# Ordering the chunked scan of a hybrid RWKV-7/Conformer layer: from a fixed tick to a rough clock of the engines

## The chip, the core and the metric

The kernel runs on one core of one Trainium2 chip. The metric is the device time of one execution in microseconds (us). The core has a matrix engine (PE, with its weight loads shown apart as PEld), a vector engine (DVE), an activation engine (ACT), a general engine (POOL) and a queue that issues transfers (SP). Each engine works through its own instructions in order, and waits on semaphores for the others.

## What is computed

One layer over 256 context tokens and 2048 latent tokens of 1024 channels. Two branches read the same normalised input, and their outputs are gated, added and projected. Cut to what matters:

```python
p = h @ w_in                                   # 74 column tiles of 128
# branch a: two linear recurrences per head (forward and backward), 16 heads of 64
def step(s, inp):
    rt, wt, kt, vt, at, bt = inp
    sa = einsum('bhij,bhj->bhi', s, at)
    s_new = s * wt + sa[..., None] * bt + vt[..., None] * kt
    return s_new, einsum('bhij,bhj->bhi', s_new if inclusive else s, rt)
y_sum = y_forward + y_backward
y_a = (layernorm_per_head(y_sum) * lnx_w + lnx_b + bonus) * silu(g_a)
# branch b: depthwise convolution over 31 tokens
z = u * sigmoid(g); z = conv31(z) + conv_b
y_b = silu(layernorm(z)) * silu(g_b)
merged = sigmoid(m_a) * (y_a @ w_proj_a) + sigmoid(m_b) * (y_b @ w_proj_b)
x_new = x + gate * (merged @ w_out); return rmsnorm(x_new)
```

## The kernel before

The program has three parts. The first normalises the input, projects the columns that the recurrence needs, and writes its operands to DRAM; a part of the gate columns is projected there too. The third is the end of the merge and the output projection. The change is in the second part, the scan.

**The scan.** The recurrence is cut into chunks of 64 tokens. Heads go in 8 pairs, a pair has 36 chunks (the first 4 are context), forward and backward chunks go together (d = 0, 1): 288 chunks in all, in steps of 4. `chunk` (L885) is a chain of three links. PE multiplies the state `SV` with the chunk's operand into `px` (L890), and ACT copies it to `xs` (L892). PE multiplies `xs` with the inverted triangle `Tt` (L896), and ACT copies the result into `UV` (L898). PE forms the update `psy` (L912), and DVE adds it to the decayed state (L914), which the next chunk's `px` needs. The output `py` (L921, L922) is off the chain; every second chunk it is copied (ACT, L935) or added (DVE, L937) into `y`.

**What fills the waits.** `prep` prepares the next step's operands (transposes `pbk`, `pvt`, the score products `psc` and their masks). `readout` (L853), once for blocks 1, 2 and once for 0, 3 of a pair, normalises `y`, and loads `bo`, `vn`, `ga` on SP. `filler` gives one dense matmul of 512 columns at a time (`pg`, L359: the rest of the gate and convolution inputs), and its own rule gives convolution steps (L969 to L977, on DVE) at `NCV` = 2.2 for every 6 matmuls. When all of that is out, `conv_branch` takes over: norms, then the projection of branch b (`pp`, L1142), then, once the last pair's blocks 1 and 2 are read out, the first projection of branch a.

**What sets the order.** A counter. `chunk` and the main loop call `tick` nine times a chunk, at fixed places:

```python
want = min(cnt["n"] * NF // NEND, NF)
while cnt["done"] < want:
    next(fill, None)
    cnt["done"] += 1
for _ in range(CBN):
    if cbs:
        next(cbs[0], None)
```

so every place gets its even share of the 2600 filler steps until the tick that 82% of 288 x 8 gives, and after that up to 3 steps of `conv_branch` (`CBN`). Every third tick takes a piece of `prep`. `readout` is a plain function, written out whole behind its chunk. Behind the code a scheduler of the build moves instructions on each engine within a short distance, with the written order as its priority; the rows of the program's order below are what it made of each version.

## Time and profile before

| what | before |
|---|---|
| median of 3 runs (lowest to highest) | 4161.96 us (4157.28 to 4163.86) |
| the profiled execution: its own time, its span | 4172.02 us, 4170.3 us |
| PE busy, PEld busy | 3840.2 us (92%), 2300.7 us (55%) |
| DVE busy, ACT busy, POOL busy | 2950.2 us (71%), 2178.5 us (52%), 352.0 us (8%) |
| mean granted clock of PE | 0.960 of full |

The span runs from the first to the last instruction. Busy time is the time in which at least one instruction of an engine was under way. A matmul is shown from its start to its modelled end, and the next one starts long before that end.

### The profile page before, as it was taken

Reading aid. Unit: us, or ns where it says so; the run is one execution under the profiler, and the core shown is the slowest. Engines: PE = TensorE matmul, PEld = TensorE weight load, DVE = VectorE, ACT = ScalarE, POOL = GpSimd, SP = SyncE. Lnnn points to the kernel's source line nnn. Section 1 sums busy time; section 2 is a strip of 40 time slices with the busy share of each in tenths; the row PEclk is TensorE's granted clock in tenths of the full one; section 3 lists DMA queues with packets and bytes.
Section 4 is the critical chain, followed back from the end, with each engine's and each line's share of the span. In section 5 each row is a group of like instructions: output and inputs, shape, how many; then the busy total and the mean of one; then the engine's idle time right before and its main releaser. Section 6 shows DMA issues by size and latency. Waiting matters only on the chain. (4 is left out here: it accounts for less than half of the span.)

```text
span 4170.3 us, 78335 instructions
## 1 busy us (share of the span) xinstructions
PE 3840.2 (92%) x29008; PEld 2300.7 (55%) x29008; DVE 2950.2 (71%) x7226; ACT 2178.5 (52%) x4358; POOL 352.0 (8%) x874
## 2 busy tenths in 40 slices
PE   8999999998999997999999999999999898788999
PEld 3444444444444443776666667666666566675444
DVE  5577787788788686877887998895466773234644
ACT  5666665666666553445454454545555553335522
POOL 0000000000000000211111111111111000010000
PEclk9999999999999998999999999999999899699999
DMA  5343443444444343444334343446455554343522
GB/s 203 124 174 138 162 152 137 146 142 168 142 150 167 121 142 106 88 92 112 82 95 109 91 119 73 109 113 156 109 124 166 146 148 118 69 91 107 199 101 76
DMA packets 586117, 528.69 MB, mean 127 GB/s; under 512 B 375044, under 2 KB 439940, under 8 KB 585224
## 3 DMA queue, kind: packets, MB, share of 16 engines
q1 hardware_dynamic: 585736, 523.68, 43.5%
q8 instruction: 231, 3.78, 0.4%
q14 instruction: 150, 1.23, 0.1%
HBM read 298.01 MB, written 196.35 MB: 119 GB/s over the span
## 5 line engine op out<-in xcount | busy, mean ns | idle before, releaser
L359 PE MATMUL pg<-hH,whi 128*128 128x512 f16 x1536 | 592.9, 386 | 11.0 <-ACT whi L199 7.1
L359 PE MATMUL pg<-hH,wlo 128*128 128x512 f16 x1536 | 591.5, 385 | 1.4 <-DVE wlo L200 1.4
L359 PE MATMUL pg<-hL,whi 128*128 128x512 f16 x1536 | 592.1, 386 | 0.0
L914 DVE SCALAR_TENSOR_TENSOR SV<-psy,PL,pre 64x64 f32<-64x64 f32 x1120 | 316.4, 283 | 232.0 <-PE psy L912 211.2
L359 PEld LDWEIGHTS <-whi 128*128 128x128 f16 x3072 | 300.5, 100 | 267.7 <-issue 45.2
L904 POOL TENSOR_SCALAR pre<-SV,PL 128x128 f32<-128x128 f32 x560 | 285.3, 509 | 1863.9 <-DVE SV L914 1771.7
L892 ACT ACTIVATE xs<-px 128x256 f32<-128x256 f32 x288 | 110.1, 382 | 439.2 <-PE px L890 437.6
L977 DVE SCALAR_TENSOR_TENSOR acc<-z,cw,acc 128x512 f32<-128x512 f32 x464 | 331.2, 754 | 2.7
L208 PE MATMUL pg<-hH,whi 128*128 128x512 f16 x832 | 318.5, 384 | 4.2 <-ACT hH L278 4.1
L209 PE MATMUL pg<-hL,whi 128*128 128x512 f16 x832 | 318.8, 383 | 0.0
L210 PE MATMUL pg<-hH,wlo 128*128 128x512 f16 x832 | 318.5, 383 | 0.0
L842 PE MATMUL psc<-arz,bk 64*128 64x128 f32 (+1 forms) x2304 | 278.7, 297 | 12.5 <-ACT UV L836 8.5
L842 PEld LDWEIGHTS psc<-arz,bk 64*128 64x128 f32 x2304 | 228.9, 196 | 85.3 <-issue 47.7
L890 PE MATMUL px<-SV,arz 128*128 128x128 f32 x1152 | 230.0, 305 | 34.0 <-DVE SV L914 29.1
L845 DVE TENSOR_TENSOR arz<-psc,msk 64x256 f32<-64x256 f32 x288 | 120.7, 419 | 168.5 <-PE psc L842 164.5
L896 PE MATMUL px<-xs,Tt 128*128 128x128 f32 x1152 | 198.1, 295 | 40.7 <-ACT xs L892 40.1
L898 ACT ACTIVATE UV<-px 64x128 f32<-64x128 f32 x576 | 154.9, 269 | 150.8 <-PE px L896 147.1
L359 PEld LDWEIGHTS <-wlo 128*128 128x128 f16 x1536 | 153.0, 100 | 137.9 <-issue 23.6
L890 PEld LDWEIGHTS px<-SV,arz 128*128 128x128 f32 x1152 | 176.1, 199 | 93.1 <-DVE SV L914 31.0
L912 PE MATMUL psy<-UV,BK 128*128 128x128 f32 x1120 | 198.9, 301 | 28.8 <-ACT UV L898 28.6
L896 PEld LDWEIGHTS px<-xs,Tt 128*128 128x128 f32 x1152 | 166.3, 199 | 89.3 <-ACT xs L892 77.3
L921 PE MATMUL py<-arz,SV 128*128 128x128 f32 x1024 | 206.6, 285 | 4.4 <-ACT y L935 2.5
(374 smaller groups left out, 8151.4 us busy)
## 6 DMA issues: line engine op xcount, KB each, us to landing
wf<-in_w_in_dram SPq DMA_DIRECT2D x74, 512.0 KB, 3.8
arz<-arD SPq DMA_DIRECT2D x144, 256.0 KB, 4.8
bkD<-bk SPq DMA_DIRECT2D x64, 512.0 KB, 2.7
arD<-ar SPq DMA_DIRECT2D x64, 512.0 KB, 3.5
bk<-bkD SPq DMA_DIRECT2D x72, 256.0 KB, 3.8
bk<-bkD SPq DMA_DIRECT2D x144, 128.0 KB, 3.9
vvz<-vD SPq DMA_DIRECT2D x144, 128.0 KB, 2.8
lt<-loD SPq DMA_DIRECT2D x32, 512.0 KB, 4.8
```

The source lines that it names most:

```text
L208: PE.matmul(ps, whi[:, k, :], xhi(k), start=(k == 0), stop=False)
L209: PE.matmul(ps, whi[:, k, :], xlo(k), start=False, stop=False)
L210: PE.matmul(ps, wlo[:, k, :], xhi(k), start=False, stop=(k == NK - 1))
L359: PE.matmul(ps, wt[a][:, k, :], b[:, k, o:o + 512], start=(m == 0), stop=(m == 23))
L842: PE.matmul(ps[h][:, c, :ni, :], bk[hs, d, c, :], ar[hs, d, c, :ni, h, :], start=True, stop=True)
L890: PE.matmul(px[:, d, :], ar[:, d, c, 0].rearrange("p h l -> p (h l)"), SV[:, d, c, :], start=True, stop=True)
L896: PE.matmul(px[:, 2 + d, :], t[:, d, c, :], xs[:, d, :], start=True, stop=True)
L904: G.tensor_scalar(pr, SV[:, d, c, :], pl, 1.0, op0=ALU.mult, op1=ALU.mult)
L912: PE.matmul(psy, BK[:, d, c, :], UV[:, d, c, :], start=True, stop=True)
L914: V.scalar_tensor_tensor(Sn[hs, d, (c + 1) % 4, hs], psy[hs, hs], PL[hs, p, d, k + 1:k + 2], pre[d][hs, hs], op0=ALU.mult, op1=ALU.add)
L921: PE.matmul(o, SV[:, d, c, :], ar[:, d, c, 1].rearrange("p h l -> p (h l)"), start=True, stop=True)
L977: V.scalar_tensor_tensor(o, x[:, j:j + 512], cw[:, 2 * j + e:2 * j + e + 1], q if j == 0 else o, op0=ALU.mult, op1=ALU.add)
```

## The change

The code of every operation stays; where it is written changes.

- **A clock.** `Clocked` wraps PE, ACT and DVE while the program is written. It keeps a time in ns for each engine and a ready time for each tile, from a rule for each kind of instruction. It does not run on the chip.
- **Dense matmuls by need.** `tick` is gone. Behind each link `until(tile)` takes filler steps while PE's clock stands before the time at which the link's tile is ready, up to 30 (`MAXP`), and at most 24 steps ahead of the even share (`AHEAD`); behind each chunk the share is made up to 12 behind (`BEHIND`). The share now ends at 82% of the chunks: chunk 236, where it was tick 1889 of nine a chunk, chunk 210. `conv_branch` gives at least 16 steps a chunk (`MINCB`) and more where `until` asks.
- **y one chunk later.** `outputs` writes a chunk's `py` behind the next chunk's `px`.
- **Convolution behind state updates.** `conv_steps(lim)` writes convolution steps while DVE's clock is less than `lim` past PE's: 3200 behind the state update, 1200 and 500 in the other two links.
- **Readout and prep in pieces.** `readout` is a generator, one piece twice a chunk; `prep` yields after each copy of `SV` and `UV`.
- Smaller: `GF` 4 to 6 (which gate tiles come between the convolution's), weight tiles of the filler loaded further ahead, norm steps in `conv_branch` only while ACT's and DVE's clocks allow.

```diff
+            def call(*a, **kw):
+                aps = [q for q in list(a) + list(kw.values()) if is_ap(q)]
+                out, ins = (kw["out"], aps) if "out" in kw else (aps[0], aps[1:])
+                t = max([clk[self._n]] + [rdy.get(key(q), 0.0) + 35 for q in ins if wrt.get(key(q)) != self._n])
...
+                    d = (165 + 0.85 * n if ps else 90 + 1.06 * n) if self._n == "act" else 200 + 1.04 * n
+                    clk[self._n] = t + d - (90 if n > 64 else 0)
+                    rdy[key(out)] = t + d + 17
+                return fn(*a, **kw)
...
+    V, S, PE = Clocked(V, "dve"), Clocked(S, "act"), Clocked(PE, "pe")
...
     def chunk(p, k, e, t):
...
         S.activation(xs, px[:, 0:2, :], AF.Copy)
-        for _ in range(3):
-            tick()
+        scores_out()
+        if c == 0 and prv[0] is not None:
+            next(prv[0], None)
+        until(xs)
+        conv_steps(LIMA)
         for d in range(2):
             PE.matmul(px[:, 2 + d, :], t[:, d, c, :], xs[:, d, :], start=True, stop=True)
...
+        pieces(2 * c)
+        conv_steps(LIMB)
+        until(UV)
...
+        conv_steps(LIM)
+        pieces(2 * c + 1)
+        until(Sn)
...
+    def conv_steps(lim):
+        while convs and clk["dve"] < clk["pe"] + lim:
+            if next(convs[0], 1) == 1:
+                convs.pop(0)
+                cv["n"] += 1
...
-    def tick():
...
+    def pull():
+        if cbs:
+            cnt["cb"] += 1
+            return next(cbs[0], 1) is None
+        if cnt["done"] >= min(cnt["n"] * NF // NEND + AHEAD, NF):
+            return False
+        cnt["done"] += 1
+        next(fill, None)
+        return True
+
+    def until(t):
+        n = 0
+        while clk["pe"] < rdy.get(key(t), 0.0) + 35 and n < MAXP and pull():
+            n += 1
+
+    def pieces(gap):
+        if rd and next(rd[0], 1) == 1:
+            rd.pop(0)
+        want = max(0, gap - 1) * NPC // 6
+        while prv[0] is not None and cnt["pc"] < want:
+            cnt["pc"] += 1
+            next(prv[0], None)
```

Three places in the order of the program show what moves. In the changed version PE, ACT and DVE instructions of the scan all carry the line of the wrapper (L822).

The first is PE in chunk 124, in the middle of the scan; `pg` with its LDWEIGHTS is a dense filler matmul. Before, from the chunk's first link on:

```order
L890 MATMUL px<-SV_18651,arz_18649 128x128 x2
L359 LDWEIGHTS wlo
L359 MATMUL pg<-hH,wlo 128x512
L359 LDWEIGHTS whi
L359 MATMUL pg<-hH,whi 128x512
L359 LDWEIGHTS whi
L359 MATMUL pg<-hL,whi 128x512
L359 LDWEIGHTS wlo
L359 MATMUL pg<-hH,wlo 128x512
L896 MATMUL px<-xs,Tt_18647 128x128 x2
```

And in the changed version:

```order
L822 MATMUL px<-SV_18651,arz_18649 128x128 x2
L822 MATMUL py<-arz_18648,SV_18650 128x128
L822 MATMUL py<-sc,UV 128x128
L822 MATMUL py<-arz_18648,SV_18650 128x128
L822 MATMUL py<-sc,UV 128x128
L822 LDWEIGHTS whi
L822 MATMUL pg<-hL,whi 128x512
L822 MATMUL px<-xs,Tt_18647 128x128 x2
```

The four `py` of the chunk before now stand in the first link, which keeps one of its four dense matmuls; the third link, where `py` stood, has six where it had four.

The second is PE in chunk 268, late in the scan (the last pair), where `conv_branch` is what is left to fill with. Before, the whole chunk:

```order
L890 MATMUL px<-SV_18651,arz_18649 128x128 x2
L921 MATMUL py<-arz_18649,SV_18651 128x128
L896 MATMUL px<-xs,Tt_18647 128x128 x2
L912 MATMUL psy<-UV,BK 128x128 x2
L922 MATMUL py<-sc,UV 128x128
L921 MATMUL py<-arz_18649,SV_18651 128x128
L922 MATMUL py<-sc,UV 128x128
```

The changed version, the first rows of the same chunk (`pp` is the projection of branch b):

```order
L822 MATMUL px<-SV_18651,arz_18649 128x128 x2
L822 MATMUL py<-arz_18648,SV_18650 128x128
L822 MATMUL py<-sc,UV 128x128
L822 MATMUL py<-arz_18648,SV_18650 128x128
L822 MATMUL py<-sc,UV 128x128
L822 MATMUL px<-xs,Tt_18647 128x128 x2
L822 LDWEIGHTS wHb
L822 MATMUL pp<-xhi,wHb 128x512
L822 LDWEIGHTS wHb
L822 MATMUL pp<-xlo,wHb 128x512
L822 LDWEIGHTS wLb
L822 MATMUL pp<-xhi,wLb 128x512
```

A chunk that held no dense matmul now holds 12 of `pp`: 5 before `psy`, and 7 behind it in the link of the state update.

The third is ACT where the second pair's blocks 0 and 3 are read out (chunk 72); `sqy` is the readout's variance tile, and a table load goes before its logarithm and before its exponential. Before, up to the `xs` that the chain waits for:

```order
L858 ACTIVATE y<-pc 128x512
L866 ACT_TABLE_LOAD
L866 ACTIVATE sqy<-sqy 128x512
L860 ACTIVATE sqy<-y 128x512
L199 ACTIVATE whi<-wf,p2s 128x1024
L877 ACTIVATE y<-y,par 128x512
L863 ACT_TABLE_LOAD
L863 ACTIVATE sqy<-pv,eps 128x512
L829 ACTIVATE BK<-pbk 128x512
L866 ACT_TABLE_LOAD
L866 ACTIVATE sqy<-sqy 128x512
L892 ACTIVATE xs<-px 128x256
```

And in the changed version:

```order
L822 ACTIVATE xs<-px 128x256
L822 ACTIVATE UV<-px 64x2x64 x2
L822 ACT_TABLE_LOAD
L822 ACTIVATE sqy<-pv,eps 128x512
L822 ACT_TABLE_LOAD
L822 ACTIVATE sqy<-sqy 128x512
L822 ACTIVATE wjk,wss<-wf 128x1024
L822 ACTIVATE BK<-pbk 128x512
L822 ACTIVATE xs<-px 128x256
L822 ACTIVATE y<-y,par 128x512
L822 ACT_TABLE_LOAD
L822 ACTIVATE sqy<-pv,eps 128x512
```

The block ahead of one `xs` has come apart into two or three, with links of the chain between them; the operations and the table loads are the same in number.

## Rows read from the trace of the kernel before

**Rows 1.** The page: span and instructions.

```profile
span 4170.3 us, 78335 instructions
```

**Rows 2.** Windows: stretch, length, busy (instructions) of PE, PEld, DVE, ACT, POOL; clock.

```profile
1675.00:3145.00 1470.00, 1389.60 (x9045) 994.25 (x9045) 1165.67 (x2794) 720.17 (x1704) 220.01 (x431) 0.98 0.45 106
3145.00:3490.00 345.00, 316.79 (x1817) 203.09 (x1815) 226.24 (x516) 179.05 (x397) 29.02 (x61) 0.95 0.56 146
3490.00:3806.00 316.00, 257.15 (x1434) 211.62 (x1434) 121.13 (x356) 137.73 (x340) 35.74 (x88) 0.83 0.43 99
3806.00:4170.00 364.00, 344.82 (x1605) 161.52 (x1603) 188.54 (x424) 130.88 (x295) 1.50 (x4) 0.98 0.36 121
```

**Rows 3.** Windows for tile px alone, PE, PEld, ACT: PE's count is eight a chunk.

```profile
1675.00:3145.00 1470.00, 297.36 (x1665) 238.67 (x1666) 191.44 (x624) 0.98 0.45 106
3145.00:3490.00 345.00, 45.87 (x256) 38.76 (x255) 29.30 (x96) 0.95 0.56 146
3490.00:3806.00 316.00, 80.09 (x352) 60.23 (x352) 40.58 (x132) 0.83 0.43 99
2511.00:2587.00 76.00, 15.89 (x96) 13.08 (x96) 11.06 (x36) 1.00 0.35 74
```

**Rows 4.** Timeline of PE at 2300 us: start, time, line, operation, count.

```profile
2299.73 0.50 PE L842 MATMUL psc<-arz,bk 64*128 64x128 f32 x6
...
2302.23 0.38 PE L359 MATMUL pg<-hH,wlo 128*128 128x512 f16 x1
...
2302.45 0.38 PE L359 MATMUL pg<-hH,whi 128*128 128x512 f16 x1
...
2309.69 0.39 PE L921 MATMUL py<-arz,SV 128*128 128x128 f32 x2
...
2311.88 0.61 PE L890 MATMUL px<-SV,arz 128*128 128x128 f32 x4
```

**Rows 5.** Windows for tile pg alone: the scan's first stretch, twelve steady chunks, three readouts.

```profile
1675.00:3145.00 1470.00, 668.34 (x2424) 21.93 (x58) 48.64 (x71) 0.98 0.45 106
2511.00:2587.00 76.00, 39.53 (x147) 2.35 (x6) 2.06 (x3) 1.00 0.35 74
2100.30:2133.00 32.70, 13.08 (x48) 0.75 (x2) 0.69 (x1) 1.00 0.49 126
2158.40:2195.00 36.60, 15.04 (x50) 0.00 (x0) 1.37 (x2) 0.86 0.48 131
2361.20:2396.00 34.80, 13.73 (x50) 0.75 (x2) 0.69 (x1) 1.00 0.43 106
```

**Rows 6.** Windows for tile pp alone: the scan's two later stretches, and behind it.

```profile
3145.00:3490.00 345.00, 187.88 (x768) 23.97 (x32) 0.95 0.56 146
3490.00:3806.00 316.00, 8.22 (x35) 0.75 (x1) 0.83 0.43 99
3806.00:4170.00 364.00, 167.25 (x735) 23.25 (x31) 0.98 0.36 121
```

**Rows 7.** Timeline at a readout: PE's px, and ACT until its copy xs.

```profile
2167.53 0.49 PE L890 MATMUL px<-SV,arz 128*128 128x128 f32 x2
...
2170.36 1.28 ACT L863 ACT_TABLE_LOAD   x1
...
2174.68 0.37 ACT L892 ACTIVATE xs<-px 128x256 f32<-128x256 f32 x1
```

**Rows 8.** Groups by line: busy, mean ns of one, idle before and its releasers.

```profile
L977 DVE SCALAR_TENSOR_TENSOR acc<-z,cw,acc 128x512 f32<-128x512 f32 x464 | 331.2, 754 | 2.7
...
L836 ACT ACTIVATE SV<-pvt 64x256 f32<-64x256 f32 x288 | 108.9, 378 | 67.1 <-PE pvt L833 61.7 <-POOL z L991 0.9 <-POOL pre L904 0.7
...
L937 DVE TENSOR_TENSOR y<-py,y 64x128 f32<-64x128 f32 x256 | 73.8, 288 | 18.3 <-PE py L922 13.8 <-issue 0.4
...
L935 ACT ACTIVATE y<-py 64x128 f32<-64x128 f32 x256 | 69.5, 272 | 114.9 <-PE py L922 112.2
```

**Rows 9.** Transfers of the scan: size each, us from issue to landing.

```profile
arz<-arD SPq DMA_DIRECT2D x144, 256.0 KB, 4.8
```

More of the change, by code (lines that the diff above doesn't have):

```diff
@@ L41 @@
 NEARLY = 21
-NCV = 2.2
+LIM = 3200
+LIMA = 1200
+LIMB = 500
+LIMN = 500
+AHEAD = 24
+BEHIND = 12
+MAXP = 30
+MINCB = 16
+NPC = 12
 TFL = (2, 1, 2, 3)
-GF = 4
+GF = 6
 NT = 8
@@ L50 @@
 RS = 1
-CBN = 3
 YS = 8
@@ L940, in chunk @@
-        tick()
+        last.append((p, k, e))
+        if k == NCH - 1:
+            return
+        pre = []
+        for d in range(2):
+            pr = bp.tile([P, P], F32, name="pre", bufs=2)
+            pl = PL[:, p, d, k + 1:k + 2]
+            G.tensor_scalar(pr, SV[:, d, c, :], pl, 1.0, op0=ALU.mult, op1=ALU.mult)
+            pre.append(pr)
+        pieces(2 * c)
+        conv_steps(LIMB)
+        until(UV)
+        Sn = SVs[(p * 9 + (k + 1) // 4) % NAR]
+        for d in range(2):
+            psy = pS.tile([P, P], F32, name="psy")
+            PE.matmul(psy, BK[:, d, c, :], UV[:, d, c, :], start=True, stop=True)
+            for hs in H2:
+                V.scalar_tensor_tensor(Sn[hs, d, (c + 1) % 4, hs], psy[hs, hs], PL[hs, p, d, k + 1:k + 2], pre[d][hs, hs], op0=ALU.mult, op1=ALU.add)
+            if d == 0:
+                s0_ = rdy[key(Sn)]
@@ L1033, in first @@
             def first():
-                if n + 2 < len(tl):
-                    w1.append(load_w1(tl[n + 2][2], wp2, WB2))
+                if not w1 and nw[0] < len(tl):
+                    w1.append(load_w1(tl[nw[0]][2], wp2, WB2))
+                    nw[0] += 1
             def chore(pr):
@@ L1046, in ahead @@
             def ahead(npr):
-                second()
+                if not w2:
+                    second()
                 for _ in range(npr):
@@ L1051, in ahead @@
                 yield
+                if tl[n + 1:] and tl[n + 1][0] == "wu" and nm != "wg":
+                    second()
+                    first()
+                    yield
             if nm == "wu":
                 wu = wt
-                for _ in ahead(0):
-                    pass
-                yield
+                if not w2:
+                    for _ in ahead(0):
+                        pass
+                    yield
                 continue
@@ L1146, in proj, with ready @@
         return ps, un
+    def ready(t):
+        for _ in range(9):
+            if clk["pe"] < rdy.get(key(t), 0.0) + 35:
+                yield
     def conv_norm(i, tmp):
@@ L1160, in conv_norm @@
                 yield
+        yield from ready(mu)
         pm = pG.tile([P, 512], F32, name="pmu", tag="pG")
@@ L1174, in conv_norm @@
                 yield
+        yield from ready(qs)
         pv = pG.tile([P, 512], F32, name="pva", tag="pG")
@@ L1273 @@
     NF = (8 * NSUB + 1) * NK + 4 * NSUB * len(gates)
-    NEND = int(TPC * 4 * NSTEP * FEND)
-    cnt = dict(done=0, n=0)
+    NEND = int(4 * NSTEP * FEND)
+    cnt = dict(done=0, n=0, pc=0, cb=0)
     prv = [None]
     cbs = []
-    def tick():
-        cnt["n"] += 1
-        if SWP == 0 and prv[0] is not None and cnt["n"] % PST == 0:
-            next(prv[0], None)
-        want = min(cnt["n"] * NF // NEND, NF)
-        while cnt["done"] < want:
-            next(fill, None)
-            cnt["done"] += 1
-        for _ in range(CBN):
-            if cbs:
-                next(cbs[0], None)
-        if SWP == 1 and prv[0] is not None and cnt["n"] % PST == 0:
+    rd = []
+    def pull():
[17 more added lines that the diff above has]
+            cnt["pc"] += 1
             next(prv[0], None)
@@ L1305 @@
             chunk(p, k, e, Tt[g % NTT])
-            tick()
+            cnt["n"] += 1
+            if cbs:
+                while cnt["cb"] < MINCB:
+                    cnt["cb"] += 1
+                    next(cbs[0], None)
+                cnt["cb"] = 0
+            else:
+                while cnt["done"] < cnt["n"] * NF // NEND - BEHIND and pull():
+                    pass
             if cnt["n"] >= NEND and cb is None:
@@ L1322 @@
                 pass
+    scores_out()
+    for r in rd:
+        for _ in r:
+            pass
     while "first" not in c_:
```

165 lines of the change are left out of this document (99 added, 66 removed).

## The prediction

> **What bounds the kernel now.** The span is 4170.3 us [rows 1]; the profiled execution's own time is 4172.0, 10 above the median of the runs, so a sum made against the profile is lowered by 10 at the end. All that the change moves lies between the scan's first `px` at 1675 us and the end. I read first the windows of the scan [rows 2]: PE is busy for 1389.6, 316.8 and 257.2 us of 1470, 345 and 316, so 167 us of 2131 are idle. That is not what can be won, since a matmul is shown to its end while the next is under way. So I count work. The timeline gives the distance between starts [rows 4]: two dense matmuls begin 0.22 us apart (2302.23, 2302.45), and two more fp32 matmuls of 128 columns make a group 0.22 us longer (0.39 for two, 0.61 for four), 0.11 each. A `psc` costs some 0.05 (six in 0.50, of which the last one's tail is about 0.28).
>
> A chunk has 8 `px`, 4 `psy` (none in the last of 36) and 8 `py` (none in the first four), 19 on average at 0.11, and of `prep` 4 transposes at about 0.11 and 8 `psc` at 0.05: 2.9 us, 3.0 with the small ones. A readout of two blocks has matmuls of 512 columns, 3.5 us by their columns. The chunks are counted by `px`, the dense matmuls by `pg` and `pp`:
>
> - 1675 to 3145: 1665/8 = 208 chunks [rows 3], 2424 `pg` [rows 5], ten readouts. Work 208 x 3.0 + 2424 x 0.216 + 35 = 1183 of 1470 us: 287 lost, 1.4 a chunk.
> - 3145 to 3490: 32 chunks [rows 3], 768 `pp` [rows 6], two readouts. Work 96 + 166 + 12 (readouts, last `pg`) = 274 of 345: 71 lost, 2.2 a chunk.
> - 3490 to 3806: 44 chunks [rows 3], 35 `pp` [rows 6], three readouts. Work 132 + 8 + 10 = 150 of 316: 166 lost, 3.8 a chunk. Here there is nothing to fill with, and the granted clock is 0.83 [rows 2].
>
> So 524 us of the scan are waits, switches and slow clock. Twelve steady chunks show how low it gets under the old order: 96/8 chunks with 147 `pg` in 76 us [rows 3, 5], work 36 + 31.8 = 67.8, 8.2 lost, 0.7 a chunk. Three steps with a readout show the other end [rows 5]: 32.7, 36.6 and 34.8 us with 48, 50, 50 `pg`, work 12 + 3.5 + 10.4 to 10.8 = 25.9 to 26.3, 6.8, 10.3 and 8.5 lost. Less 4 x 0.7 that is 5.7 a readout. Why is in the timeline [rows 7]: `px` starts at 2167.53, and ACT copies it at 2174.68, after the readout's work with its table loads of 1.28 us.
>
> The Trainium skill (Perfetto Trace Analysis, Identifying the Most-Contended Engine) says that matmul busy time is no measure of the headroom, because pipelined matmuls overlap. By busy time at most 167 us were to be had in the scan; by the count 524. The trace sides with the page: 0.38 us a matmul, 0.22 between starts [rows 4].
>
> **The change, part by part.** Work is the same: the same matmuls, copies, transfers and table loads. Each term is a part of the 524 us.
>
> *The share ends at chunk 236, and `conv_branch` gives by need.* Before, the 768 `pp` of branch b went out in 32 chunks, most at 24 to 27 each, then 44 chunks had almost none. In the order of the changed program the 42 chunks from 240 to 281 hold 744 of them, 16 in most, and the six behind them none. These 76 chunks lose 237 us now. With matmuls in every chunk I put them at the 1.4 of the first stretch, which has all kinds of chunks in it: 106, so **-131**. Bounds: 0.7 a chunk (53, -184) and the 2.2 of the stretch in which `conv_branch` ran beside the chain (167, -70).
>
> *The last six chunks are bare, and the first projection of branch a comes behind the scan.* Before, it covered the last four chunks; now blocks 1 and 2 are read out in pieces over some eight chunks, and its 192 matmuls follow the last `px`. That moves work, and adds six bare chunks at 3.8 - 1.4 = 2.4, 14 us, and, as an estimate between 0 and twice that, 8 us of waiting for the readout and the input's split: **+22**. Bounds +10 and +40.
>
> *Readout in pieces.* Ten readouts lie in the first stretch, 57 us. In the order ACT's block of eleven operations ahead of one `xs` becomes two of about six, and each link has its own matmuls to hide some. Half goes: **-28**. Bounds 0 and -57. Its loads `bo`, `vn`, `ga` and the store move with it on SP, one or two steps further among `prep`'s loads.
>
> *Dense matmuls per link, y, convolution: the ordinary chunks.* The four `py` (0.9 us) now stand in the first link, in place of most of its dense matmuls, and the third link has more of these in their place. Counted over both orders at the distances above, a first link holds 1.2 us of other work on average (1.0 before), a second 1.0 (1.2) and a third 1.9 (2.0): cover is moved, not added. For the change speaks that it is put where the clock sees a wait. Against it stand three things. On ACT 180 of the 256 copies of `y` now stand between `xs` and `UV`, where none stood: 0.272 us each, 49 us [rows 8]; in exchange only 70 of the 244 copies of `prep` at 0.378 that stood there remain, 66 us less. On DVE 61 state updates of 279 stand straight behind a convolution step of 0.754 us [rows 8], 84 before; but the steps now come in bursts: in runs of twelve updates 18 to 68 of them, where it was 37 to 68, each run of many at the old peak. Third, fills are bunched: 37 of the first 240 chunks hold under 4 us of work, 21 before. I put the sum at **0**. Bounds: the 84 us that the first stretch loses beyond 0.7 a chunk and the readouts (287 - 146 - 57) all go, -84; or 0.6 a chunk more, the 2.0 that the stretch beside `conv_branch` comes near to, 208 x 0.6 = +125.
>
> *The transfers of `prep`.* `arz` of the next step waits until the old one's last `py`, which is now a chunk later. It lands 4.8 us after its issue [rows 9], and its first reader `psc` stands in the step's second or third chunk, 6 us and more behind. **0**; if that cover were gone, up to 4.8 in each of 71 steps.
>
> Sum: -131 + 22 - 28 + 0 = -137. 4172 - 137 = 4035; less 10, 4025 us, 3.3% below the median.
>
> **The rivals.**
>
> 1. *Every chunk becomes a steady one.* For it speaks that 12 chunks in a row reach 0.7. Then -184 - 57 - 84 + 22 = -303: 3859 us. Against it: the clock knows nothing of transfers, of slow stretches of PE's clock or of the scheduler behind it. 0.12.
> 2. *Only the thin end is won.* The rough times are off often enough that matmuls stand where no wait is; bunches leave bare chunks, readouts cost what they did: -70 + 22 + 0, and some +10: about -40, 4122 us. For it: 37 bare chunks in the order. 0.15.
> 3. *Slower: y's adds hold PE.* `py` has one buffer. The adds of 64 groups of four go to DVE (256 adds [rows 8], four a group), where steps of 0.754 us stand ahead of them, written up to 3.2 us past PE's time. `py` is now in the first link, so a `py` that waits for an add of the pair before holds `px` behind it and with it the chain. From 137/64 = 2.1 us a group on, three convolution steps, the gain is gone; at five steps, 3.8 us, it is +243 - 137 = +106, 4268 us. Against it: a whole chunk of 5 to 8 us lies between the `py` that closes a pair and the one that opens the next. 0.08.
> 4. *No effect.* The scheduler of the build undoes the placing, and the thin end shifts from one place to another: within 0.2% of 4162. Against it: its own order shows `pp` in the late chunks. 0.05.
>
> **How the numbers follow.** The forecast, 4025 us, has 0.60; its own range, by half of the bounds of its terms, is 3970 to 4085. The range that should hold the time takes in rival 2 and the better half of what lies towards rival 1, and leaves out about 0.1 at either end: 3930 to 4130. A measurement of this kernel can't tell less than 0.2% from no change, the spread of its three runs. Faster by more: 0.60 + 0.12 + 0.15 = 0.87; within: 0.05; slower: 0.08.
>
> **What would show it.** In the profile after: no stretch of 40 chunks without dense matmuls, the last third of the scan at 8 us a chunk with a granted clock above 0.95 (right), or chunks of 9 and more there (the 1.4 is wrong); the scan's first 208 chunks at 1380 us (1470 less the 28 of the readouts and the 278 `pg`, 60 us, that the order moves to later chunks); the longest waits of `xs` for `px` at a readout 3 to 5 us where it was 7; the last six chunks at 4 to 5 us each with a low clock. The prediction is wrong if ordinary chunks lose over 2 us each (rival 2), if `py` waits for DVE in the table of waits (rival 3), or if waits of `UV` behind copies of `y` are among the longest.

## The result, and the profile after

The changed kernel takes 4115.8 us, median of 4 runs (4103.8 to 4116.9), against 4160.1 us for the kernel before in the same session: ratio 0.9886, 95% interval 0.9866 to 0.9907. It is faster by 44 us (1.1%), where the prediction had 137. The profiled execution has a span of 4114.1 us, 56 less than that of [rows 1]. First two rows of the page after, the span and the busy time by engine:

```profile
span 4114.1 us, 78249 instructions
PE 3802.2 (92%) x29008; PEld 2254.8 (55%) x29008; DVE 2950.5 (72%) x7226; ACT 2181.7 (53%) x4356; POOL 356.8 (9%) x874
```

The windows of the scan after, cut at the same chunks as [rows 2] where that is possible: chunks 0 to 207, 208 to 239, 240 to 280, 281 to 286, and from the last chunk's first `px` to the end. Columns as in [rows 2], with the mean granted clock behind POOL:

```profile
1676.00:3107.00 1431.00, 1339.92 (x8744) 963.15 (x8744) 1123.52 (x2689) 694.10 (x1658) 221.98 (x430) 0.97 0.45 102
3107.00:3336.00 229.00, 214.82 (x1355) 154.21 (x1353) 128.92 (x355) 134.90 (x307) 27.98 (x61) 0.97 0.56 142
3336.00:3707.00 371.00, 339.12 (x2032) 224.37 (x2033) 239.40 (x565) 186.72 (x420) 36.85 (x82) 0.94 0.51 127
3707.00:3743.00 36.00, 30.03 (x186) 24.77 (x185) 17.98 (x50) 21.04 (x45) 4.12 (x10) 0.91 0.51 183
3743.00:4114.00 371.00, 346.75 (x1583) 157.82 (x1582) 192.70 (x431) 134.55 (x305) 0.00 (x0) 0.97 0.40 131
```

And the same stretches for `pg` alone (they answer to [rows 5]) and for `pp` alone (to [rows 6]):

```profile
1676.00:3107.00 1431.00, 557.38 (x2146) 21.83 (x58) 40.97 (x60) 0.97 0.45 102
3107.00:3336.00 229.00, 77.65 (x303) 0.00 (x0) 8.87 (x13) 0.97 0.56 142
...
3336.00:3707.00 371.00, 181.86 (x740) 22.48 (x30) 0.94 0.51 127
3707.00:3743.00 36.00, 1.23 (x5) 0.75 (x1) 0.91 0.51 183
3743.00:4114.00 371.00, 169.90 (x768) 23.99 (x32) 0.97 0.40 131
```

The stretch of 41 chunks without dense matmuls is gone: 740 `pp` lie in chunks 240 to 280. These chunks take 9.0 us each at a clock of 0.94, where the prediction wanted 8 at above 0.95, and the first 208 take 1431 us for its 1380. To see what was won I count as the prediction did, elapsed time less PE's work, but with the number of every matmul of each chunk from the program's order and the distances of [rows 4], for both kernels (before, that gives 509 us lost up to the last chunk, where the prediction's simpler count had 524):

| chunks | before: us, work, lost | after: us, work, lost |
|---|---|---|
| 0 to 207 | 1470, 1191, **279** | 1431, 1127, **303** |
| 208 to 239 | 345, 280, **66** | 229, 177, **53** |
| 240 to 280 | 282, 133, **149** | 371, 296, **76** |
| 281 to 286 | 58, 43, **15** | 36, 21, **15** |
| from the last `px` | 340 | 371 |

The distances of [rows 4] make this count too wide by some 50 us in the first 208 chunks of either kernel. The six `psc` in 0.50 us from which the prediction took 0.05 each are the end of a group of sixteen, which starts at 2299.07 and takes 1.16 us, and in which they go in pairs. A group of eight can take as long (in the timeline after):

```profile
2378.59 1.16 PE L822 MATMUL psc<-arz,bk 64*128 64x128 f32 x8 [0.53 <-ACT sqy L822]
```

By the starts in the traces 476 and 480 pairs of `psc` lie 0.007 us apart there, and 744 and 736 stand alone, 0.11 apart (an estimate: 137 and 136 us for the 85 that 0.05 each gives). As it is the same in both, the differences stand.

The late chunks lose 87 us less. The first 208 lose 24 more, although the prediction took 28 off. The part behind the scan is 31 us longer. 25 of it are `pp`: 768 lie there now, and before 651, as the window from its last `px` on shows; the 117 of difference take 0.216 us each. So some 6 us are left for the waiting that the prediction estimated at 8.

```profile
3831.00:4170.00 339.00, 147.24 (x651) 21.00 (x28) 0.98 0.36 120
```

Where do the first chunks lose more? Among the costliest are those in which the second block of a readout is normalised: eight such chunks (the 32nd of a pair) lose 2.9 to 8.4 us each. Here is one, chunk 103, in the timeline after, ACT first and then DVE (start, length, operation, count, in brackets the idle time ahead and what ended it):

```profile
2376.16 0.38 ACT L822 ACTIVATE xs<-px 128x256 f32<-128x256 f32 x1
2376.55 1.28 ACT L822 ACT_TABLE_LOAD   x1
2377.85 0.69 ACT L822 ACTIVATE sqy<-pv,eps 128x512 f32<-128x512 f32 x1
2378.56 0.77 ACT L822 ACTIVATE SV<-pvt 64x256 f32<-64x256 f32 x2
2379.35 1.28 ACT L822 ACT_TABLE_LOAD   x1
2380.64 0.63 ACT L822 ACTIVATE sqy<-sqy 128x512 f32<-128x512 f32 x1
2381.18 0.54 ACT L822 ACTIVATE UV<-px 64x128 f32<-64x128 f32 x2
...
2376.53 0.75 DVE L822 SCALAR_TENSOR_TENSOR y<-ga,gUga,y 128x512 f32<-128x512 f32 x1
2381.30 0.69 DVE L822 TENSOR_TENSOR y<-y,sqy 128x512 f32<-128x512 f32 x1 [4.02 <-ACT sqy L822]
2382.03 0.43 DVE L822 TENSOR_TENSOR arz<-psc,msk 64x256 f32<-64x256 f32 x1
```

`xs` ends at 2376.54 (2376.16 + 0.38), and `UV`, the next link, is copied at 2381.18: between them stand a table load, the logarithm, a copy of `prep`, another table load and the exponential, though the readout was cut up so that links of the chain come between its pieces. DVE stands still for 4.02 us: at the head of its queue is `y` times `sqy`, which waits for that exponential, and behind it the masks of `prep`. Then PE is at half clock. Its rows just behind, in the same timeline:

```profile
2382.92 2.07 PE L822 MATMUL psc<-arz,bk 64*128 64x128 f32 x8
2384.92 0.61 PE L822 MATMUL pg<-hH,wlo 128*128 128x512 f16 x1
2385.32 0.63 PE L822 MATMUL pg<-hH,whi 128*128 128x512 f16 x1
2385.75 0.63 PE L822 MATMUL pg<-hL,whi 128*128 128x512 f16 x1
...
2388.43 0.38 PE L822 MATMUL pg<-hH,wlo 128*128 128x512 f16 x1
2388.64 0.61 PE L822 MATMUL px<-SV,arz 128*128 128x128 f32 x4
```

Two `pg` are 0.43 us apart where [rows 4] has 0.22, and the next `px` waits behind ten of them. The window of these 7.5 us has a granted clock of 0.54, so nearly all of it is at 1.2 GHz:

```profile
2381.00:2388.50 7.50, 6.73 (x22) 4.07 (x23) 4.72 (x11) 2.43 (x7) 1.14 (x2) 0.54 0.29 62
```

The table of waits after, for the two things that the prediction named as signs of a slower kernel, and for the engine pairs of the chain (us in total, times, longest):

```profile
ACT xs L822 <- PE px L822: 380.6, 164, 10.4
ACT UV L822 <- PE px L822: 206.0, 188, 7.6
DVE y L822 <- ACT sqy L822: 42.4, 22, 4.0
PE pbk L822 <- DVE sc L822: 23.8, 19, 6.8
PE py L822 <- DVE y L822: 1.2, 2, 0.7
```

`py` waits for `y` for 1.2 us in all: the rival with DVE's adds is out. New is that `prep`'s transposes `pbk` wait for DVE's masks, once for 6.8 us (before, 2.5 us in all).

### The profile page after: what moved, and what is told of

Its sections match the earlier page's. It is cut to its first block, busy times and chain, and to the rows that moved or that the text cites. A ratio compares the mean times of both kernels' runs of the same rounds, so it can differ in the third digit from the quotient of the medians.

```text
span 4114.1 us, 78249 instructions
## 1 busy us (share of the span) xinstructions
PE 3802.2 (92%) x29008; PEld 2254.8 (55%) x29008; DVE 2950.5 (72%) x7226; ACT 2181.7 (53%) x4356; POOL 356.8 (9%) x874
## 5 line engine op out<-in xcount | busy, mean ns | idle before, releaser
L822 DVE SCALAR_TENSOR_TENSOR SV<-psy,PL,pre 64x64 f32<-64x64 f32 x1120 | 315.8, 282 | 187.7 <-PE psy L822 168.1
L822 PE MATMUL pg<-hH,whi 128*128 128x512 f16 x864 | 336.1, 389 | 5.7 <-ACT whi L822 4.0
L822 PE MATMUL pg<-hH,wlo 128*128 128x512 f16 x864 | 335.6, 388 | 0.4 <-DVE wlo L822 0.3
L822 PE MATMUL pg<-hL,whi 128*128 128x512 f16 x864 | 335.8, 389 | 0.0
L822 DVE SCALAR_TENSOR_TENSOR acc<-z,cw,acc 128x512 f32<-128x512 f32 x464 | 331.7, 757 | 2.7
L822 ACT ACTIVATE xs<-px 128x256 f32<-128x256 f32 x288 | 109.3, 380 | 383.1 <-PE px L822 381.5
L822 PE MATMUL psc<-arz,bk 64*128 64x128 f32 (+1 forms) x2304 | 259.5, 293 | 14.7 <-ACT UV L822 7.1
L822 ACT ACTIVATE UV<-px 64x128 f32<-64x128 f32 x576 | 156.1, 271 | 211.7 <-PE px L822 207.0
L822 PEld LDWEIGHTS <-whi 128*128 128x128 f16 x1728 | 172.8, 101 | 149.7 <-issue 20.2
L822 PEld LDWEIGHTS psc<-arz,bk 64*128 64x128 f32 x2304 | 211.7, 192 | 65.9 <-issue 13.3
L822 PE MATMUL px<-SV,arz 128*128 128x128 f32 x1152 | 222.8, 297 | 24.8 <-DVE SV L822 22.9
L822 PEld LDWEIGHTS px<-SV,arz 128*128 128x128 f32 x1152 | 181.9, 195 | 84.5 <-issue 29.3
L822 PE MATMUL psy<-UV,BK 128*128 128x128 f32 x1120 | 200.4, 300 | 25.6 <-ACT UV L822 23.2
L822 PE MATMUL px<-xs,Tt 128*128 128x128 f32 x1152 | 194.7, 292 | 29.4 <-ACT xs L822 28.3
L822 DVE TENSOR_TENSOR arz<-psc,msk 64x256 f32<-64x256 f32 x288 | 120.5, 419 | 140.7 <-PE psc L822 137.1
```

Source lines behind the costliest of these rows:

```text
L822: return fn(*a, **kw)
```

## The experiments

Seventeen kernels were timed, four to six runs each, next to the kernel before, which had medians of 4159 to 4165 us. Ratios are to it, with the 95% interval. "Changed" stands for the kernel after the change, and what is said of one edit is against its 4116 us unless it says otherwise.

**First round: which part made the gain, which took it back.** One kernel has the late stretch alone, in the old code; three undo one part of the change each.

Late stretch alone (all else as before):

```diff
-CBN = 3
+CBN = 2
-    NEND = int(TPC * 4 * NSTEP * FEND)
+    NEND = int((TPC + 1) * 4 * NSTEP * FEND)
```

> The kernel before, with the even share ending at chunk 236 instead of 210, and two steps of conv_branch a tick instead of three; its ticks, y, convolution and readout stay. In its order 740 pp stand in chunks 240 to 280, 741 in the changed kernel's. Theory A (the gain comes from the late stretch alone, and the new order of the ordinary chunks gives about 24 us of it back): chunks 208 to 286 lose some 86 us less than before, chunks 0 to 207 the old 1.3 a chunk on fewer matmuls, so 4160 - 80 = 4080 us, faster than the changed kernel by 36. Rival B (the whole of the change's gain is the late stretch, the rest is neutral, as the prediction has it): 4116, like the changed kernel. Rival C (matmuls placed by need made the late stretch good): 4130 or more.

Measured: 4067.1 us, 0.9772 (0.9750 to 0.9794). That is 97 us less than before and 49 less than the changed kernel. The windows of chunks 240 to 280 and of the whole scan of this kernel:

```profile
3307.00:3669.00 362.00, 335.03 (x2051) 224.64 (x2049) 243.35 (x569) 195.44 (x433) 35.09 (x79) 0.98 0.54 137
1673.00:3700.00 2027.00, 1909.10 (x12315) 1365.76 (x12315) 1513.26 (x3658) 1032.03 (x2429) 286.36 (x583) 0.98 0.48 116
```

The clock there is 0.98 where the changed kernel has 0.94. Theory A holds, and more strongly than it said: two changed numbers do better than the whole change.

Dense matmuls by an even share in each link, not by the clock (the rest as changed):

```diff
     def until(t):
-        n = 0
-        while clk["pe"] < rdy.get(key(t), 0.0) + 35 and n < MAXP and pull():
-            n += 1
+        cnt["t"] += 3
+        want = min(cnt["t"] * NF // (9 * NEND), NF)
...
+            while cnt["done"] < want:
+                cnt["done"] += 1
+                next(fill, None)
```

> The changed kernel, but the dense matmuls by an even share in each of the three links (three ninths of a chunk each, six conv_branch steps a link), not by the clock; y, convolution, prep and readout as changed. Rival B (placing by the clock is worth something): slower, 4130 to 4145. Theory A with the dense matmuls' bunches as the cause of the 24 us: 4090. Theory A with the convolution's bursts as the cause: same within 8 us, 4108 to 4124.

Measured: 4066.9 us, 0.9774 (0.9751 to 0.9797), 49 us less. By the count above the first 208 chunks lose 270 us for 303, chunks 208 to 286 127 for 144. The placing by the clock costs, and more than any of the three forecasts had; nearest is the one that blames the matmuls' bunches, with 4090.

Convolution spread evenly, four steps behind each state update:

```diff
-        while convs and clk["dve"] < clk["pe"] + lim:
+        n = 4 if lim == LIM else 0
+        while convs and n > 0:
+            n -= 1
```

> The changed kernel, but four convolution steps behind each chunk's state update and none elsewhere, whatever the clocks say. Theory A1 (convolution written in bursts makes DVE late for prep's masks and for state updates, and holds the PSUM tiles of prep): the 24 us come back, 4116 - 24 = 4092; PE's waits of pbk for the masks fall from 23.8 us to under 8, and the state update's longest delays go. Theory A2 (the loss is in y or in the matmuls' bunches): same within 8 us.

Measured: 4115.3 us, 0.9886 (0.9867 to 0.9906): no difference. The bursts of convolution, which I had named as the likeliest cause from the new waits of `pbk`, cost nothing that can be measured. Theory A1 falls. The waits of `pbk` for the masks stay as well, at 20.2 us, so they don't come from the bursts.

Readout whole behind its chunk, in the changed kernel:

```diff
+            if k in (27, 35):
+                scores_out()
+                for _ in readout(p, *((1, 2) if k == 27 else (0, 3))):
+                    pass
```

> The changed kernel with each readout written out whole behind its chunk, as before the change. The prediction's term (pieces are worth 28 us over ten readouts): 4116 + 28 to 40 = 4144 to 4156. Theory A3 (a readout in pieces costs what it did, since the pieces stand so close that the table loads and the wait of DVE for the exponential still fall into two or three chunks): same within 8 us, with the chunks k = 35 to 6 worse by about 19 us in the first five pairs and the chunks k = 27 to 34 better by about 16.

Measured: 4087.2 us, 0.9829 (0.9807 to 0.9851), 28 us less. Neither theory had that: this whole readout is better than the one in pieces. The groups by line show why it may be: its ACT has 45 table loads in the wrapper's line, where the changed kernel has 71 (rows further down). The new readout has its logarithms in a loop of their own, so that written whole, both logarithms come together.

**Second round: the two losses apart.** Both undone at once; the clock kept, but each chunk held to its own share; the pieces kept, but the logarithms together; and `y` back in its own chunk.

Both undone at once:

> Both undone at once in the changed kernel: dense matmuls by an even share (alone 4067 us, 49 less than the changed kernel) and each readout whole behind its chunk (alone 4087, 28 less). If the two losses are apart: 4116 - 49 - 28 = 4039. If they are one and the same (the clock misplaces matmuls around the pieces, so either edit alone heals it): 4060 to 4075. Thin end alone with the old code had 4067: below it, something else of the change is worth having.

Measured: 4054.7 us, 0.9748 (0.9724 to 0.9772): between the two answers, 12 us better than even shares alone.

Each chunk held to its own share:

```diff
-AHEAD = 24
-BEHIND = 12
-MINCB = 16
+AHEAD = 11
+BEHIND = 0
+MINCB = 18
...
         if cbs:
+            if cnt["cb"] >= 18:
+                return False
```

> The changed kernel; the clock still chooses the link, but each chunk gets its own even share and no more (no more than 11 steps ahead, none behind, 18 of conv_branch a chunk). The spread of dense matmuls over the first 208 chunks falls from 6.6 to 3.9 (3.8 in the version with even fills). Theory S (the loss of the clock comes from matmuls bunched across chunks, which leaves others bare and PE at half its clock): near the even version, 4067 to 4080. Theory L (the loss is in the choice of the link, a first link of under 1 us of other work in 155 of 201 chunks): same as the changed kernel, 4108 to 4124.

Measured: 4074.6 us, 0.9788 (0.9765 to 0.9810), 41 us less. The choice of the link by the clock may stay. Theory S holds here, by which a chunk that takes another one's matmuls is what costs; but the edit also shortens the runs of matmuls in a link, and the dose below parts the two.

Readout still in pieces, but its two logarithms next to each other:

```diff
             S.activation(sq, pv, AF.Ln, scale=1.0 / 64, bias=eps[:, 2:3])
-            yield
```

> The changed kernel with the readout's two logarithms in one piece with each other and the two exponentials behind them, so that 134 table loads stand in ACT's order instead of 162, all other pieces apart as changed. Theory T (what a readout in pieces costs are its table loads, 1.28 us each, one before each logarithm and each exponential, where the whole readout has 26 fewer): 28 loads are 36 us of ACT, and as with the whole readout about 28 us come back, 4085 to 4095. Theory P (it is the pieces' place in the links): same, 4108 to 4124.

Measured: 4071.8 us, 0.9781 (0.9758 to 0.9804), 44 us less from one word taken out. The groups by line (count, busy, mean ns), before, changed, with the readout whole, and here:

```profile
L863 ACT ACT_TABLE_LOAD x32 | 41.1, 1283 | 0.6
L866 ACT ACT_TABLE_LOAD x31 | 39.8, 1283 | 0.5
```

```profile
L822 ACT ACT_TABLE_LOAD x71 | 91.1, 1283 | 1.3
```

```profile
L822 ACT ACT_TABLE_LOAD x45 | 57.7, 1283 | 0.8
```

```profile
L822 ACT ACT_TABLE_LOAD x43 | 55.2, 1283 | 0.7
```

28 loads are gone, 36 us of ACT, and the time falls by 44. By the order 60 of the 71 are the readouts', for 63 before. ACT in this kernel's timeline, in the same readout as above:

```profile
2361.66 0.36 ACT L822 ACTIVATE xs<-px 128x256 f32<-128x256 f32 x1
2362.83 0.55 ACT L822 ACTIVATE UV<-px 64x128 f32<-64x128 f32 x2 [0.80 <-PE px L822]
2363.40 1.28 ACT L822 ACT_TABLE_LOAD   x1
2364.70 1.26 ACT L822 ACTIVATE sqy<-pv,eps 128x512 f32<-128x512 f32 x2
2365.98 1.28 ACT L822 ACT_TABLE_LOAD   x1
2367.28 1.15 ACT L822 ACTIVATE sqy<-sqy 128x512 f32<-128x512 f32 x2
```

One load now serves both logarithms and one both exponentials, in one block between `UV` and the next `xs`, in the link that has the most other work. Theory T holds, with more than the 20 to 30 us that it forecast. PE's clock goes along: it is at half for 79 us between the scan's first and last `px`, where the changed kernel has 143. So the 44 us need not all be time of ACT.

This run also stands against the whole readout above: 45 and 43 loads, 4087 us whole and 4072 in pieces. With even shares it is 4055 whole and, in the next round, 4036 in pieces. Where the logarithms come together, then, the pieces gain 15 and 19 us, in both cases with intervals that don't overlap.

Even shares, and `y` in its own chunk:

> The version with even fills (4067 us), and a chunk's y again behind its own state update instead of behind the next chunk's first link. The prediction's term (0): 4059 to 4075. If y one chunk later helps, because the four py fill the first link: 4080 to 4100. If its copies ahead of UV cost (180 copies of 0.27 us): 4030 to 4050.

Measured: 4080.1 us, 0.9805 (0.9784 to 0.9825): 13 us more than with `y` one chunk later, at the near edge of what the second theory forecast. So that part of the change is worth some 13 us under even shares, though the two intervals overlap a little; with `y` back the first 208 chunks take 1417 us, for 1394.

**Third round: do they add up, and does a better clock help?** First each chunk's own share and the logarithms together:

> The changed kernel with each chunk's own share (alone 4075 us, 41 less) and the readout's logarithms and exponentials together (alone 4072, 44 less). If the two losses are apart: 4116 - 41 - 44 = 4031. If both act through the same thing, PE's clock falling to half behind a chunk with too few matmuls (139 us of the scan at half clock in the changed kernel, 75 and 79 in the two edits): no further gain than the better of the two, 4060 to 4075, with about 75 us at half clock again.

Measured: 4039.7 us, 0.9708 (0.9685 to 0.9732): 76 us less, of the 85 that the two edits have alone. PE is at half clock for 44 us, where the second theory expected about 75. They are two losses, not one.

Then even shares and the logarithms together:

> Even shares in each link instead of the clock (alone 4067 us) and the readout's logarithms and exponentials together (134 to 136 table loads for 162). If the two are apart: 4067 - 44 = 4023. If the readout costs little once its chunks have their even share: 4050 to 4067. Below 4050 it is the fastest version so far, with y one chunk later (worth 13 us) and the late stretch filled.

Measured: 4035.8 us, 0.9693 (0.9670 to 0.9715), the fastest median of the study, 3.1% below before, and between the two answers. The first 208 chunks and chunks 240 to 280 of this kernel:

```profile
1671.00:3056.00 1385.00, 1292.88 (x8734) 940.06 (x8733) 1127.01 (x2693) 672.37 (x1643) 227.06 (x430) 0.99 0.47 105
...
3282.00:3628.00 346.00, 328.64 (x2041) 219.64 (x2042) 235.90 (x562) 183.04 (x418) 39.62 (x82) 0.98 0.55 135
```

46 and 25 us shorter than in the changed kernel, at a clock of 0.99 and 0.98 for 0.97 and 0.94.

The rough clock with the table loads in it:

```diff
+                    if self._n == "act":
+                        fs = {AF.Ln: 1, AF.Exp: 2, AF.Tanh: 2}.get(a[2] if len(a) > 2 else None, 0)
+                        if fs and fs != clk["tab"]:
+                            clk["tab"] = fs
+                            d += 1283
```

> The changed kernel, but the rough clock counts 1.28 us of ACT for each change between logarithm, exponential and the rest, which it leaves out. If the clock misplaces matmuls because it does not know the table loads: 4075 to 4095, near the versions with even shares. If it is the freedom to run ahead or behind that costs, whatever the clock knows (24 steps ahead, 12 behind): same, 4108 to 4124. In the order the spread over the first 208 chunks stays at 6.6.

Measured: 4102.4 us, 0.9855 (0.9834 to 0.9877): 13 us less, short of the 4075 to 4095 of the first theory and just under the second one's. What the clock does not know of the loads is a small part of its cost at most; the intervals of this run and of the changed kernel overlap.

**Fourth round: is it PE's clock?** Between the scan's first and last `px` PE is at half clock for 143 us in the changed kernel, and for 67 with even shares, summed over the profiler's record of the granted clock. So I filled thin chunks with matmuls that no output needs.

```diff
         until(Sn)
+        if cb is None and cnt["done"] - cnt["d0"] < 9:
+            for _ in range(2 * (9 - cnt["done"] + cnt["d0"])):
+                PE.matmul(px[:, 0:2, :], hH[:, 0, 0:P], hH[:, 0, 0:2 * P], start=True, stop=True)
```

> The changed kernel with added work that no output needs: in each of the first 236 chunks that gets fewer than 9 dense matmuls, matmuls of 256 columns into the free half of px fill up the difference behind the state update, 648 in 93 chunks, 70 us of columns at full clock, 0.75 us a chunk. Chunks with few matmuls lose over 1 us each, so most of it should find a wait to lie in. Theory H (what the uneven shares cost is PE's clock, which falls to half behind chunks with few matmuls: 93 us at half clock in chunks 0 to 239, against 31 with even fills): the half-clock time falls to under 50 us, and the time by 10 to 30, to 4086 to 4106. Theory W (it is the waits of the bare links themselves, the half clock only goes with them): half clock may fall, the time does not: 4116 to 4150. At 4186 none of the added work is hidden.

Measured: 4134.1 us, 0.9932 (0.9910 to 0.9954), 18 us more. Of 70 us of added work 52 vanish in waits, so the thin chunks do have waits to fill; but PE was still at half clock for 68 us in the first 240 chunks (92 in the changed kernel), and the time did not fall. Theory H had asked for under 50 and a lower time: it is not confirmed, and not excluded either, since the half clock fell about half as far as it asked.

**Fifth round: parting the readout's two changes, and the dose.** First the loads without pieces, in the late stretch alone with the old whole readout:

```diff
-            pv = pC.tile([P, 512], F32, name="pv", tag="pC")
-            PE.matmul(pv, bones, sq, start=True, stop=True)
-            S.activation(sq, pv, AF.Ln, scale=1.0 / 64, bias=eps[:, 2:3])
             rs.append(sq)
         for sq in rs:
+            pv = pC.tile([P, 512], F32, name="pv", tag="pC")
+            PE.matmul(pv, bones, sq, start=True, stop=True)
+            S.activation(sq, pv, AF.Ln, scale=1.0 / 64, bias=eps[:, 2:3])
+        for sq in rs:
             S.activation(sq, sq, AF.Exp, scale=-0.5)
```

> The thin end alone in the old code (4067 us), with the readout still whole, but its variances and logarithms in a loop behind the squares of both blocks, so that the two logarithms come next to each other and 136 table loads stand in ACT's order for 162. Theory T (every load between chain copies costs, about 1.1 to 1.6 us each as in the pieces): 4067 - 28 to 44 = 4023 to 4039. Theory P (loads cost only in pieces; in a whole readout they are one block in any case): 4059 to 4075.

Measured: 4039.1 us, 0.9707 (0.9690 to 0.9725): 28 us less than the late stretch alone, at the edge of theory T, and level with the best version that has the rest of the change. Its table loads, and its windows of the first 208 chunks and of chunks 240 to 280:

```profile
L865 ACT ACT_TABLE_LOAD x18 | 23.1, 1283 | 0.3
L867 ACT ACT_TABLE_LOAD x18 | 23.1, 1283 | 0.3
```

```profile
1674.00:3053.00 1379.00, 1314.59 (x8743) 951.27 (x8744) 1125.56 (x2689) 665.35 (x1637) 218.91 (x431) 1.00 0.46 106
...
3280.00:3640.00 360.00, 334.74 (x2047) 222.71 (x2046) 242.87 (x567) 190.32 (x428) 36.10 (x79) 0.98 0.53 136
```

Then pieces against whole at equal loads: the changed kernel with the readout of before, whole, each logarithm behind its own square (71 loads again).

> The changed kernel with the readout exactly as before the change: whole behind its chunk, each block's logarithm behind its own square, 162 table loads as in the changed kernel. If the pieces, at equal loads, are worth what the prediction gave them (28 us): 4116 + 20 to 35 = 4136 to 4151. If cutting up is worth nothing and the gain of the whole readout of e4 was its loads: 4108 to 4124. If wholeness itself is better: 4087 as in e4.

Measured: 4114.3 us, 0.9880 (0.9859 to 0.9901): the same. In the first 208 chunks the whole readout loses 314 us for 303, so that the pieces may have 11 there; late chunks and tail take it back, since in pieces blocks 1 and 2 are read out later and branch a starts later. At 71 loads, cutting the readout up is worth nothing in all; at 43 to 45 it gained 15 and 19 us. In this run PE is at half clock for 109 us of the scan, for 143 in the changed kernel, and the time is the same.

And twice the freedom of the dense matmuls (`AHEAD` 48, `BEHIND` 24), then half of it (17 and 6), then the same freedom with at most 8 in a row (`MAXP` 8 for 30):

> The changed kernel with twice the freedom of the dense matmuls: 48 steps ahead of the even share and 24 behind, for 24 and 12. Their spread over the first 208 chunks becomes 9.6 for 6.6, and 19 of these chunks have none, for 9. If unevenness is the cause of the 41 us that the even share of each chunk gave back: slower, 4116 + 20 to 60 = 4136 to 4176, with more than 79 us at half clock in chunks 0 to 207. If it is not: 4108 to 4124.

Measured: 4118.0 us, 0.9890 (0.9868 to 0.9911): the same. The spread over the chunks is not what the time goes by; theory S falls in its plain form.

> The changed kernel with 17 steps ahead of the even share and 6 behind, for 24 and 12; the spread over the first 208 chunks becomes 5.5 (6.6 in the changed kernel, 3.9 where each chunk has its own share). If the uneven shares cost from some size on and are saturated at 24: between the two, 4085 to 4105. If only an exact share helps: 4108 to 4124. If half suffices: 4075.

Measured: 4105.9 us, 0.9866 (0.9845 to 0.9886), 10 us less, with overlapping intervals: unclear, if anything a small gain.

> The changed kernel, with its freedom of 24 and 12, but at most 8 dense matmuls (1.7 us) in a row by the clock in one link, for 30; the rest of a chunk's share is written behind the chunk. It spreads conv_branch over all late chunks too, up to the last. If long runs are what costs (22 third links of the first 200 chunks hold over 3 us of other work and lose 1.17 us each): 4116 - 26 or more, 4070 to 4090. If it is the shares between chunks (spread 5.3): 4085 to 4105 as e16. If neither: 4108 to 4124.

Measured: 4076.6 us, 0.9793 (0.9769 to 0.9817), 39 us less. At nearly the same spread as the run before (5.3 and 5.5) it gains four times as much, so long runs cost more than uneven shares do. In the first 208 chunks it loses 23 us less; the other 16 us lie in the late ones. Counted in the program's order, the links of the first 208 chunks that hold 12 dense matmuls or more (2.6 us), beside what these chunks lose by the count above:

| kernel | links of 12 and more | lost, us |
|---|---|---|
| before | 10 | 279 |
| late stretch alone | 7 | 273 |
| even shares | 10 | 270 |
| runs of 8 at most | 17 | 280 |
| share per chunk | 18 | 277 |
| half freedom | 25 | 297 |
| changed | 34 | 303 |
| twice the freedom | 37 | 302 |

All but the kernel before have the new late stretch, and all have 69 to 73 table loads from the scan on. Among them the loss goes with the count of long links, which may be why twice the freedom cost nothing: the count hardly rises. Fewer loads lower the loss at the same count: the changed kernel with its logarithms together has 42 such links by the starts in its trace, and its first 208 chunks take 1400 us for 1431. In the late chunks the count alone does not explain it. In these the even share, the share per chunk and the short runs all cure two chunks, 259 and 271, that lose 13.2 and 7.9 us in the changed kernel and 0.3 to 5.7 in these three; 259 has almost no `pp` while DVE and ACT work through a norm of `conv_branch`.

## Why the prediction was wrong

The sum was -137 us and the time fell by 44. Against its steps:

- **The share ends at chunk 236, `conv_branch` by need: -131, and +22 for the last chunks and branch a.** Together -109. The late stretch alone gave 97, so mechanism and size hold; its own count is 96 us less lost in chunks 208 to 286, the bare six included. The clock's version of it gave 87, and its chunks 240 to 280 lose 1.9 us each, for the 1.4 of the sum. Of the +22 the six bare chunks lose 15 us in 36, at a clock of 0.91, and some 6 us of waiting lie behind the scan.
- **Readout in pieces: -28.** This step failed. At the loads of the change, pieces and whole take the same time (4116 and 4114; some 11 us gained in the first 208 chunks are lost behind them). I read the seven microseconds ahead of `xs` in [rows 7] as a block to be cut, and noted that operations and table loads stay the same in number. That was so, and it was the point: the loads stay, 1.28 us each, one ahead of each logarithm and each exponential, and cut up they land ahead of two or three links instead of one. What was to be had first is their number: 26 fewer gave 28 us in the old whole readout, and 28 fewer 44 in the changed one, 1.1 and 1.6 us a load. With them PE's half clock fell too, from 68 to 31 us and from 143 to 79, and no run parts the two. With the loads fewer, the pieces bring 15 and 19 us after all, of the 28.
- **Ordinary chunks: 0.** This is the step that failed most. I had added up covers (1.0, 1.2 and 2.0 us a link before and after) and called it moved, not lost. The mean was the wrong number to look at: the clock makes 34 links of 12 dense matmuls and more out of 10, and what stands there is missing in others. Its placing costs 39 to 49 us (even shares, share per chunk, runs of 8). The three things that I held against the change were weighed wrongly: the fills as the clock bunches them cost that much, the convolution's bursts nothing (4115 us without them), and `y` one chunk later gains some 13.
- **`prep`'s transfers: 0.** In the table of waits 0.2 us are put down to the transfer of `arz`. It stands.
- **The count itself.** A `psc` at 0.05 us was the price of one in a pair, so the 524 us of losses hold over 50 us of `psc` work. And half of the bounds of the terms, added up, give 3936 to 4141 us, not the 3970 to 4085 of the forecast's own range.

In a ladder of medians: before 4164; late stretch alone 4067; with readout and `prep` in pieces, convolution by the clock and the smaller edits 4080; with `y` one chunk later 4067; with the dense matmuls by the clock 4116. Against the terms that is 12 us less from the late stretch, 41 from the second step (28 forecast, 13 lost) and 36 from the ordinary chunks. The 13 us of the second step stay unresolved between its parts, as pieces and convolution each showed nothing alone. It was rival 2, which I gave 0.15, with the two sizes wrong: a late stretch of 97 for its 48, and a cost of the clock of 40 to 50 where it had 10. Its sign, the 37 thin chunks in the order, had been counted and not priced.

What stays open is how the long runs cost. A chunk with few matmuls has waits, and 52 us of added work lay hidden in them. PE is also longer at half clock: for 143 us in the changed kernel, 67 with even shares, 79 with a share per chunk, 106 with short runs. As a dense matmul takes 0.43 us there for 0.22, half of such a stretch is lost at most. If it costs alike in all of them, then of the 49, 41 and 39 us that these three give the clock carries up to 38, 32 and 19, an estimate. No run here shows how it divides: the added work took 24 us of half clock away and the time rose, and the readout of before took 34 away and the time stayed, but both also changed what the waits hold.

The Trainium skill (ScalarE: Activation LUTs, What ACT_TABLE_LOAD costs) gives a switch of tables 1.28 us for the load and 1.38 us of drain. The trace agrees on the first (1283 ns, all loads) and shows nothing of the second: the load starts 0.01 us behind the end of `xs` (2376.16 + 0.38, 2376.55), the logarithm 0.02 behind the load's end. By the total of that section of the Trainium skill, 26 and 28 loads would be worth 69 and 74 us, an estimate from its 2.66 us a switch; the runs have 28 and 44.

## What to carry to other kernels

Before a burst of work is cut into pieces, look at what in it is a fixed price for each switch: two activation functions that need different tables cost a load each time that they alternate, so group the same functions first, and only then place the group. Here cutting the burst up paid nothing with the loads as they were, and 15 and 19 us with them grouped. Where matmuls are placed by an estimate of the engines' times, judge the order by its tails and not by its mean: count the links with far more cover than a wait has, and those with none. And try the plainest part of a large change alone: two numbers for the end of an even share and the grouping of the logarithms reach what the best version with all the rest does, 4039 and 4036 us.

## What the runs showed that I had not expected

- A logarithm and the exponential behind it never shared a table here: 31 and 29 loads stand ahead of them in the changed kernel's order, for 32 of each operation, and in its trace, from the scan on, each of the 35 changes from the one to the other has a load between them. The Trainium skill (ScalarE: Activation LUTs, Table sets: the hidden batching unit) names a set that holds both, by which the pair would need one load; as this program was built, it takes two.
- Most of the work added to PE can vanish in a kernel with PE at 92%: 648 more matmuls, 70 us of columns, cost 18 us.
